# Reordering the front of a hybrid block: w_o's first two units, w_ada's last two column pairs, and which buffers short-lived tiles take

## The chip, the cores and the metric

The kernel runs on one core of a Trainium2 chip. The metric is the device time of one execution in microseconds (us). The engines are TensorE (PE: matrix products and transposes), VectorE (DVE), ScalarE (ACT), GpSimd (POOL) and SyncE (SP), which here issues nearly all the loads from HBM. Each engine works through its own list of instructions in order. An instruction that waits holds up everything behind it in that list.

## The reference, cut to what matters

The block has 256 tokens of width 1024. A conditioning vector goes through `w_ada` and gives six rows of 1024 numbers (shift, scale and gate for each half of the block). The first half is a mixer, the second a mixture of 32 experts of which each token uses four:

```python
c_act = jax.nn.silu(c)
ada = (c_act @ w_ada[l] + b_ada[l])[:, None, :]
sh_m, sc_m, g_m, sh_f, sc_f, g_f = jnp.split(ada, 6, axis=-1)
h = rms_norm(x, norm_mix_g[l]) * (1.0 + sc_m) + sh_m
...
merged = jax.nn.sigmoid(g_attn) * a_branch + jax.nn.sigmoid(g_conv) * c_branch
return merged @ w_o
...
x = x + g_m * mix
h = rms_norm(x, norm_ffn_g[l]) * (1.0 + sc_f) + sh_f
ffn = moe_ffn(h.reshape(B * S, D), router_w[l], router_b[l], ...)
x = x + g_f * ffn.reshape(B, S, D)
return rms_norm(x, norm_final_g)
```

`h` goes through one large projection `w_in` (attention latents, the inputs of a short convolution, and two gates `g_attn`, `g_conv` of 1024 columns each). `a_branch` is attention times `w_up_attn`, `c_branch` the convolution times `w_up_conv`. In `moe_ffn` the router's logits `h @ router_w + router_b` choose the experts, and every expert has `w_gu` (1024 x 2048) and `w_down` (1024 x 1024).

## The kernel before

**Two parts.** The front (the mixer up to the router and the gather for expert 0) lasts to about 242 us. After that the 32 experts follow one another. Each expert's weights are read once, as 2 MB tiles: four of `w_gu` and two of `w_down`, 12 MB for an expert.

**Buffers.** SBUF has 22 "narrow" buffers of 1 MB, numbered 0 to 21. After the front they are regarded as 11 "wide" buffers of 2 MB: wide buffer i is the narrow pair 2i and 2i+1. A wide tile can be loaded when the last reader of both its halves is done. `Slots.take` gives the buffer that was given back longest ago; `upto` (22, and 16 from unit 10 of the front on) makes it prefer the first so many. The wide tiles take the wide buffers in the order in which these were last given back, so the tiles that come last in this order are the ones whose narrow halves were in use longest.

**Loads.** SP issues all weights in one fixed order, `loads`: the front's units ("w": pieces of `w_in`, `w_up_conv`, `w_up_attn`, `w_o`, mostly 1 MB) and 16 chunks of `w_ada` of 1 MB ("a"), then the experts' tiles. `pump` issues the next load whenever more buffers are free than `spare`, and `spare` comes from a small table by unit. This fixes at which place in the program a load stands and which buffer it gets. On the chip the load then waits for that buffer's last reader, and all loads behind it wait too.

**Splitting.** Each front unit is used as two rounded parts. `split` takes two buffers, ScalarE writes the high part (L345), VectorE subtracts it from the raw weight for the low part (L346), and the raw buffer is given back. `unit()` returns the next unit and has the two after it split ahead of time. A product is then three matmuls (L334 to L336).

**w_ada in the front.** Of the sixteen chunks, (1, j) for j 0 to 7 are multiplied on TensorE (`ada_mm`, L250; 8 of them add up in one PSUM tile to row 1, which holds the mixer's gate `g_m` and the shift `sh_f`). The chunks (2, j) are multiplied and added on VectorE (L445, L448), and `ada_sum` (L455) adds over the partitions to row 2, with the scale `sc_f` and the gate `g_f`. `ada_next` handles the next chunk in the order of `ada_todo`: first all of row 1, then all of row 2.

**Order of the front after attention's scores.** Gates 4 to 7 (columns of `g_conv`) with attention in between; the convolution branch (`br`, two units); `gm_b` (`g_m` spread over the partitions, L462) and `sh_col` (the shift, transposed, L319), from which POOL computes `rwb` (router weights times shift) and VectorE its sum `rws` (L784); gates 0 to 3 (columns of `g_attn`) with an `ada_next` after each; `halves` of the attention output on ACT (L691) and POOL (L692); the attention branch's first unit, `ada_sum`, its second unit; `merge_t` (transposes of the merged branches, L799); `w_o` (`wo_mm`); the router.

**w_o.** It has four units of two row blocks each and four accumulators (two token tiles by two column halves). All four units are split before the first product. The first two units go into accumulator (0,0), then (0,1), (1,0) and (1,1); then come the router's constant terms (L934, L935, with `rws`), and the last two units, accumulator by accumulator, with the residual and the norm following each. A unit's buffers are given back (`drop`) after the last accumulator has used it.

## Time and profile before

| | us |
|---|---|
| median of 3 runs | 1167.49 (1165.46 to 1169.42) |
| the profiled execution's own time | 1166.59 |
| its span, first to last instruction | 1164.9 |
| TensorE busy in the span | 1067.3 (92%) |
| VectorE, ScalarE, GpSimd busy | 358.5, 152.8, 35.4 |
| moved by DMA | 457.66 MB, 393 GB/s over the span |

Busy shares are averages over two very different parts, the front and the experts, so the rows below go by stretch. The stretch 187 to 242 us is the front's end, 250 to 1135 us the experts.

### The profile page before, as it was taken

Reading aid. Unit: us, or ns where it says so; the run is one execution under the profiler, and the core shown is the slowest. Engines: PE = TensorE matmul, PEld = TensorE weight load, DVE = VectorE, ACT = ScalarE, POOL = GpSimd, SP = SyncE. Lnnn points to the kernel's source line nnn. Section 1 sums busy time; section 2 is a strip of 40 time slices with the busy share of each in tenths; the row PEclk is TensorE's granted clock in tenths of the full one; section 3 lists DMA queues with packets and bytes.
Section 4 is the critical chain, followed back from the end, with each engine's and each line's share of the span. In section 5 each row is a group of like instructions: output and inputs, shape, how many; then the busy total and the mean of one; then the engine's idle time right before and its main releaser. Section 6 shows DMA issues by size and latency. Waiting matters only on the chain. (4 is left out here: it accounts for less than half of the span.)

```text
span 1164.9 us, 11805 instructions
## 1 busy us (share of the span) xinstructions
PE 1067.3 (92%) x4914; PEld 488.5 (42%) x4914; DVE 358.5 (31%) x703; ACT 152.8 (13%) x261; POOL 35.4 (3%) x89
## 2 busy tenths in 40 slices
PE   5898998999999999999999879999888988898986
PEld 1887776744343343333433243343224322342323
DVE  3766688423221232122122121222112211211223
ACT  1544643311000010000000000010001000000001
POOL 1000002100000000000000000000000000000000
PEclk8898999979999999998999999999999999998999
DMA  9973686999999999999999999999999999999995
GB/s 354 393 271 136 231 325 240 352 429 429 424 430 426 428 428 415 428 428 427 428 427 429 429 423 429 427 427 429 426 428 428 428 428 428 427 428 426 428 419 180
DMA packets 48078, 457.66 MB, mean 393 GB/s; under 512 B 4939, under 2 KB 10088, under 8 KB 20628
## 3 DMA queue, kind: packets, MB, share of 16 engines
q1 hardware_dynamic: 47074, 456.06, 94.2%
q8 instruction: 41, 0.67, 0.2%
q0 software_dynamic: 272, 0.66, 0.2%
q10 hardware_dynamic: 674, 0.14, 0.1%
q14 instruction: 17, 0.14, 0.0%
HBM read 455.79 MB, written 1.05 MB: 392 GB/s over the span
## 5 line engine op out<-in xcount | busy, mean ns | idle before, releaser
L1074 PE MATMUL pg<-w,hsel 128*64 128x512 f32 x2048 | 459.4, 603 | 25.4 <-DMA w<-in_w_gu 25.2
L1074 PEld LDWEIGHTS pg<-w,hsel 128*64 128x64 f32 x2048 | 143.3, 139 | 325.9 <-issue 277.0
L1112 PE MATMUL pm<-w,aT 128*64 128x512 f32 (+1 forms) x1056 | 227.7, 582 | 9.1 <-DMA w<-in_w_down 7.6
L1092 DVE TENSOR_SCALAR ga<-pg 128x512 f32<-128x512 f32 x32 | 22.1, 692 | 459.2 <-PE pg L1074 442.4
L1112 PEld LDWEIGHTS pm<-w,aT 128*64 128x64 f32 x1056 | 74.0, 137 | 157.8 <-issue 133.9
L1093 ACT ACTIVATE sgm<-ga 128x512 f32<-128x512 f32 x32 | 20.2, 630 | 685.4 <-DVE ga L1092 685.4
L1118 DVE TENSOR_TENSOR yp<-gfx,pm 64x512 f32<-64x512 f32 x62 | 42.5, 685 | 196.5 <-PE pm L1112 195.9
L346 DVE TENSOR_TENSOR w<-w 128x2048 fp32r<-128x2048 f32 (+3 forms) x26 | 56.9, 2202 | 18.3 <-ACT w L345 18.0
L479 PE MATMUL mm<-w 128*128 128x512 f32 (+1 forms) x240 | 59.4, 408 | 2.7 <-ACT w L419 2.7
L1046 PE MATMUL pm<-oh,xs 128*128 128x256 f32 (+1 forms) x256 | 57.2, 383 | 4.7 <-DVE oh L1033 4.7
L1046 PEld LDWEIGHTS pm<-oh,xs 128*128 128x128 f32 x256 | 49.5, 200 | 15.9 <-issue 11.1
L334 PE MATMUL mm<-w 128*128 128x256 f32 (+1 forms) x160 | 54.2, 339 | 1.8 <-ACT w L691 1.2
L1137 PE MATMUL mm<-yp,s 128*128 128x512 f32 x120 | 54.9, 600 | 0.8 <-DVE yp L1118 0.8
L336 PE MATMUL mm<-w 128*128 128x256 f32 (+1 forms) x160 | 53.4, 334 | 1.7 <-DVE w L346 1.0
L479 PEld LDWEIGHTS mm<-w 128*128 128x128 f32 x240 | 48.3, 203 | 12.0 <-ACT w L419 3.8
L335 PE MATMUL mm<-w 128*128 128x256 f32 (+1 forms) x160 | 52.8, 330 | 0.0
L345 ACT ACTIVATE w<-w 128x2048 fp32r<-128x2048 f32 (+3 forms) x26 | 47.3, 1839 | 19.2 <-DMA w<-in_w_in 12.3
L1137 PEld LDWEIGHTS mm<-yp,s 128*128 128x128 f32 x120 | 22.1, 190 | 30.0 <-issue 27.5
L334 PEld LDWEIGHTS mm<-w 128*128 128x128 f32 x160 | 30.9, 193 | 8.4 <-issue 3.5
L250 PE MATMUL pa<-w,cact 128*32 128x512 f32 x128 | 21.1, 744 | 13.9 <-DVE rs_v L141 8.6
L1103 PE MATMUL pm<-ident,sgm 128*128 128x128 f32 x128 | 23.8, 308 | 10.4 <-ACT s L1066 7.9
L1223 POOL CAST sel<-id 128x256 fp32r<-128x256 f32 x32 | 12.7, 402 | 676.8 <-PE pg L1226 676.7
(283 smaller groups left out, 624.5 us busy)
## 6 DMA issues: line engine op xcount, KB each, us to landing
w<-in_w_gu SPq DMA_DIRECT2D x128, 2048.0 KB, 38.7
w<-in_w_down SPq DMA_DIRECT2D x62, 2048.0 KB, 39.1
w<-in_w_ada SPq DMA_DIRECT2D x24, 1024.0 KB, 6.5
w<-in_w_in SPq DMA_DIRECT2D x14, 1024.0 KB, 5.4
w<-in_w_o SPq DMA_DIRECT2D x4, 1024.0 KB, 9.0
w<-in_w_up_conv SPq DMA_DIRECT2D x2, 1024.0 KB
w<-in_w_up_attn SPq DMA_DIRECT2D x2, 1024.0 KB
w<-in_w_down SPq DMA_DIRECT2D x4, 512.0 KB, 32.3
```

Of the source, the lines that this page charges most:

```text
L334: TE.matmul(o, l[0], r[0], start=start, stop=False, skip_group_check=True)
L335: TE.matmul(o, l[0], r[1], start=False, stop=False, skip_group_check=True)
L336: TE.matmul(o, l[1], r[0], start=False, stop=stop, skip_group_check=True)
L345: S.activation(hi, raw, AF.Copy)
L346: V.tensor_tensor(lo, raw, hi, op=ALU.subtract)
L479: TE.matmul(ps[i][:, :n], hT[l][:, 4 * half + q, i * P:(i + 1) * P], u[r][:, q, :], start=(half == 0 and q == 0 and l == 0 and r == 0), st ...
L1046: TE.matmul(p[:, q, :], xs[:, i, fcols(2 * q2 + q)], oh[:, i, :n], start=(i == 0), stop=(i == NT - 1))
L1074: TE.matmul(pg[64 * g:64 * g + 64, n, :], hs[k // 4][:, k % 4, c0:c0 + CAP], w[:, f0:f0 + 512], start=False, stop=(k == NQ - 1), skip_grou ...
L1103: TE.transpose(p[:, q, :], a[:, q::4], ident)
L1112: TE.matmul(py[64 * h:64 * h + 64, :], aT[:, qa, 64 * g:64 * g + 64], w[:, h], start=(b == 0), stop=(b == 7), skip_group_check=True)
L1118: V.tensor_mul(yp[64 * k2:64 * k2 + 64, h * 512:(h + 1) * 512], gfx[hp, :], py[hp, :])
L1137: TE.matmul(acc[i][h], s2[:n, i * P:(i + 1) * P], yp[:n, h * 512:(h + 1) * 512], start=start, stop=False, skip_group_check=True)
```

## The change

1. `take` no longer goes by `upto` but prefers the first 16 buffers for everything that isn't a load. Once no loads are left in the list, it also prefers a buffer whose other half is held. `pump` counts only free buffers among the first `upto`, and the `spare` table is lower.
2. `ada_todo` goes (2,0), (1,0), (2,1), (1,1) and so on. SP's list of loads has the same kinds at the same places, so it is another chunk that is loaded at each "a".
3. `gm_b`, `sh_col` and `rwb` come after the attention branch; the sum `rws` after the fourth split of `w_o`.
4. `w_o`'s unit one goes into all four accumulators (with the second `merge_t` after the first two), then unit two into all four. The third unit is split after unit one's products, the fourth after unit two's. The last two units are used as before.

```diff
--- before.py
+++ after.py
@@ -79,8 +79,10 @@
             for i in range(len(since)):
                 pool.tile([P, size], F32, name="w", tag=f"w{i}", bufs=1)
 
-        def take(self, shape, dtype=F32):
-            i = min((i >= self.upto, c, i) for i, c in enumerate(self.since) if c is not None)[2]
+        def take(self, shape, dtype=F32, upto=16):
+
+            i = min((i >= upto, not loads and self.since[(i ^ 1) % len(self.since)] is not None, c, i)
+                    for i, c in enumerate(self.since) if c is not None)[3]
             self.since[i] = None
             t = self.pool.tile([P] + list(shape), dtype, name="w", tag=f"w{i}", bufs=1)
             self.held[id(t)] = (t, i)
@@ -93,7 +95,7 @@
             self.pump()
 
         def pump(self):
-            while loads and sum(c is not None for c in self.since) > self.spare:
+            while loads and sum(c is not None for c in self.since[:self.upto]) > self.spare:
                 loads.pop(0)()
 
     loads = []
@@ -365,19 +367,19 @@
         jobs += [mat_unit(w_up_attn, k) for k in range(2)]
         jobs += [mat_unit(w_o, k) for k in range(4)]
         raws, done, taken = [], [], [0]
-        ada_todo = [(g, j) for g in (1, 2) for j in range(8)]
+        ada_todo = [(g, j) for j in range(8) for g in (2, 1)]
         ada_raw, ada_ps = [], {}
 
         def ada_load(g, j):
             def issue():
-                w = slot([2048])
+                w = slot([2048], upto=narrow.upto)
                 load(w, ap_of(w_ada, g * 2048 + j * 6 * D, [[8 * 6 * D, P], [1, 2048]]))
                 ada_raw.append((g, j, w))
             return issue
 
         def raw_load(shape, src):
             def issue():
-                w = slot(shape)
+                w = slot(shape, upto=narrow.upto)
                 load(w, src)
                 raws.append((w, shape))
             return issue
@@ -398,7 +400,7 @@
         def unit():
             k = taken[0]
             taken[0] += 1
-            narrow.spare = {4: 7, 8: 6, 14: 5, 18: 4}.get(k, narrow.spare)
+            narrow.spare = {4: 6, 8: 4, 12: 3, 16: 2, 18: 1}.get(k, narrow.spare)
             if k == 10:
                 narrow.upto = 16
             ahead(k + 1 + LOOK[k])
@@ -771,17 +773,6 @@
         ada_next()
         next(br)
         ada_next()
-        gm_b = keep.tile([P, D], F32, name="gm_b", tag="bg2")
-        for h in range(2):
-            p = tpt()
-            spread_row(p, 1, h)
-            S.activation(gm_b[:, h * 512:(h + 1) * 512], p, AF.Copy)
-        V.tensor_copy(by_half(sh_col[:, 1, :]), halves_t(brow[1], tpt(), fcols)[:, 2:4, :, 0])
-        rwb = ft("rwb", [P, NE, NQ], 2, "pe0")
-        for q in range(NQ):
-            G.tensor_scalar(rwb[:, :, q], rw[:, q, :], sh_col[:, 1, q:q + 1], None, op0=ALU.mult)
-        rws = ft("rws", [P, NE])
-        V.reduce_sum(rws, rwb, axis=AX.X)
         for k in range(4):
             gate(k)
             if k == 3:
@@ -808,12 +799,21 @@
         ada_sum()
         wo = [unit(), unit()]
         next(br)
+        gm_b = keep.tile([P, D], F32, name="gm_b", tag="bg2")
+        for h in range(2):
+            p = tpt()
+            spread_row(p, 1, h)
+            S.activation(gm_b[:, h * 512:(h + 1) * 512], p, AF.Copy)
+        V.tensor_copy(by_half(sh_col[:, 1, :]), halves_t(brow[1], tpt(), fcols)[:, 2:4, :, 0])
         V.tensor_copy(by_half(a_col[:, 1, :]), halves_t(brow[2], tpt(), fcols)[:, 0:2, :, 0])
         V.scalar_tensor_tensor(a_col[:, 1, :], a_col[:, 1, :], 1.0, gffn, op0=ALU.add, op1=ALU.mult)
+        rwb = ft("rwb", [P, NE, NQ], 2, "pe0")
+        for q in range(NQ):
+            G.tensor_scalar(rwb[:, :, q], rw[:, q, :], sh_col[:, 1, q:q + 1], None, op0=ALU.mult)
+        rws = ft("rws", [P, NE])
         give(sg[1])
         mT = [slot([NQ, T], F32R), slot([NQ, T], F32R)]
         merge_t(0)
-        wo += [unit(), unit()]
         ss1 = keep.tile([P, NT, 2], F32, name="ss1")
 
         wps = [[None, None], [None, None]]
@@ -922,14 +922,20 @@
                 TE.matmul(ph[q // 4][:, q % 4, :], xs[:, i, fcols(q)], oh0[:, i, :],
                           start=(i == 0 and q % 4 == 0), stop=(i == NT - 1), skip_group_check=True)
 
-        wo_mm(0, 0, 0, 4)
-        wo_mm(0, 1, 0, 4)
+        wo_mm(0, 0, 0, 2)
+        wo_mm(0, 1, 0, 2)
         merge_t(1)
         give(sg[0])
         for q in range(NQ):
             G.tensor_scalar(rwa[:, q, :], rw[:, q, :], a_col[:, 1, q:q + 1], None, op0=ALU.mult)
-        wo_mm(1, 0, 0, 4)
-        wo_mm(1, 1, 0, 4)
+        wo_mm(1, 0, 0, 2)
+        wo_mm(1, 1, 0, 2)
+        wo.append(unit())
+        for i in range(NT):
+            for h in range(2):
+                wo_mm(i, h, 2, 4)
+        wo.append(unit())
+        V.reduce_sum(rws, rwb, axis=AX.X)
         p = tpt()
         TE.matmul(p[:, :NE], ones[0:1, :], rb, start=True, stop=False)
         TE.matmul(p[:, :NE], ones, rws, start=False, stop=True)
```

In the rows below, `w_...`, `mm_...`, `tp_...` and `pa_...` are tiles with their numbers; line numbers of the kernel after are 2 higher up to gate 0, and differ a little beyond. "x4" is four instructions.

**TensorE between the convolution branch and gate 0.** Before, the branch's last product is followed by `gm_b` (L462), `sh_col` (L319) and the gate's first products (L479):

```order
L335 MATMUL mm_1348<-w_1279,w_1217 128x512
L336 MATMUL mm_1348<-w_1278,w_1217 128x512
L462 MATMUL tp_1420<-brow12_145,ident_95 128x512
L462 MATMUL tp_1423<-brow12_145,ident_95 128x512
L319 MATMUL tp_1426<-ident_95,brow12_145 128x128 x4
L479 MATMUL mm_1443<-w_1337,w_339 128x512 x4
L479 MATMUL mm_1444<-w_1337,w_339 128x512 x4
```

Now it is followed by the chunk (1, 4) of `w_ada` (L252, raw buffer `w_1359`), and the gate:

```order
L337 MATMUL mm_1327<-w_1261,w_1204 128x512
L338 MATMUL mm_1327<-w_1260,w_1204 128x512
L252 MATMUL pa_697<-w_1359,cact_184 32x512 x4
L481 MATMUL mm_1401<-w_1316,w_339 128x512 x4
L481 MATMUL mm_1402<-w_1316,w_339 128x512 x4
L481 MATMUL mm_1401<-w_1316,w_340 128x512 x4
L481 MATMUL mm_1402<-w_1316,w_340 128x512 x4
```

`gm_b` and `sh_col` have moved behind the attention branch (L464, L321 there). A product that reads a freshly loaded chunk of `w_ada` stands in their place.

**TensorE in the first products of w_o.** Before, `w_1585` and `w_1625` (the high parts of units one and two) go into the same accumulator `mm_1705`; then the next accumulator follows:

```order
L334 MATMUL mm_1705<-w_1585,w_1668 128x512
L335 MATMUL mm_1705<-w_1586,w_1668 128x512
L336 MATMUL mm_1705<-w_1585,w_1669 128x512
L334 MATMUL mm_1705<-w_1625,w_1668 128x512
L335 MATMUL mm_1705<-w_1626,w_1668 128x512
L336 MATMUL mm_1705<-w_1625,w_1669 128x512
L334 MATMUL mm_1705<-w_1625,w_1668 128x512
L335 MATMUL mm_1705<-w_1626,w_1668 128x512
L336 MATMUL mm_1705<-w_1625,w_1669 128x512
L334 MATMUL mm_1718<-w_1585,w_1668 128x512
```

Now unit one (`w_1557`, `w_1558`) goes on to the next accumulator, `mm_1703`, and the second `merge_t` (L790) follows:

```order
L336 MATMUL mm_1696<-w_1557,w_1667 128x512
L337 MATMUL mm_1696<-w_1558,w_1667 128x512
L338 MATMUL mm_1696<-w_1557,w_1668 128x512
L336 MATMUL mm_1703<-w_1557,w_1667 128x512
L337 MATMUL mm_1703<-w_1558,w_1667 128x512
L338 MATMUL mm_1703<-w_1557,w_1668 128x512
L336 MATMUL mm_1703<-w_1557,w_1667 128x512
L337 MATMUL mm_1703<-w_1558,w_1667 128x512
L338 MATMUL mm_1703<-w_1557,w_1668 128x512
L790 MATMUL tp_1710<-ident_95,w_1403 128x128 x4
```

Unit two (`w_1601`, `w_1602`) comes after all 24 products of unit one.

**VectorE around the last splits.** Before, the low parts of units three and four (`w_1685`, `w_1689`) are made between the two `merge_t` (L803), and `rws` far ahead, before gate 0:

```order
L803 TENSOR_TENSOR w_1669<-tp_1670,w_1668 128x4x128
L803 TENSOR_TENSOR w_1669<-tp_1677,w_1668 128x4x128
L346 TENSOR_TENSOR w_1685<-w_1544,w_1684 128x2048
L346 TENSOR_TENSOR w_1689<-w_1547,w_1688 128x2048
L872 MEMSET lg_1695 128x2x8
L874 MEMSET m8_1697 128x16
L803 TENSOR_TENSOR w_1669<-tp_1731,w_1668 128x4x128
L803 TENSOR_TENSOR w_1669<-tp_1738,w_1668 128x4x128
```

Now both (`w_1747`, `w_1775`) stand behind the second `merge_t` (L794), with `rws` (L938) after them:

```order
L794 TENSOR_TENSOR w_1668<-tp_1710,w_1667 128x4x128
L794 TENSOR_TENSOR w_1668<-tp_1717,w_1667 128x4x128
L348 TENSOR_TENSOR w_1747<-w_1542,w_1746 128x2048
L348 TENSOR_TENSOR w_1775<-w_1551,w_1774 128x2048
L938 TENSOR_REDUCE rws_1666<-rwb_1657 128x32
L833 TENSOR_TENSOR jk_1795<-mm_1696,gm_b_1637 128x512
L834 TENSOR_TENSOR xs_90<-xs_90,jk_1795 128x512
```

`w_1747` is written into the buffer of `w_1558`, the low part of unit one, and `w_1775` into the buffer of `w_1601`, the high part of unit two. TensorE's product with `rws` (L941) comes right after unit two's last product, as before.

## Rows read from the trace of the kernel before

**Rows 1.** The page, the span in 40 equal slices: DMA busy tenths, GB/s.
```profile
DMA  9973686999999999999999999999999999999995
GB/s 354 393 271 136 231 325 240 352 429 429 424 430 426 428 428 415 428 428 427 428 427 429 429 423 429 427 427 429 426 428 428 428 428 428 427 428 426 428 419 180
```

**Rows 2.** The page, costliest groups of instructions: the experts' first matrix product.
```profile
L1074 PE MATMUL pg<-w,hsel 128*64 128x512 f32 x2048 | 459.4, 603 | 25.4 <-DMA w<-in_w_gu 25.2
```

**Rows 3.** Busy time by stretch: us, five engines, TensorE clock, DMA share, GB/s.
```profile
187.00:197.00 10.00, 8.27 (x33) 6.00 (x34) 8.43 (x9) 0.00 (x0) 0.00 (x0) 0.83 0.00 2
197.00:213.00 16.00, 15.44 (x76) 11.88 (x75) 8.80 (x13) 5.98 (x7) 9.02 (x12) 1.00 0.92 326
213.00:228.00 15.00, 14.77 (x77) 11.65 (x76) 6.95 (x22) 4.78 (x10) 0.00 (x0) 1.00 1.00 379
228.00:250.00 22.00, 17.98 (x87) 11.79 (x87) 9.17 (x32) 5.29 (x10) 3.97 (x6) 0.69 0.97 397
250.00:280.00 30.00, 30.00 (x150) 13.66 (x148) 7.34 (x24) 5.67 (x9) 0.40 (x1) 1.00 1.01 428
600.00:1135.00 535.00, 484.05 (x2092) 178.55 (x2089) 111.08 (x214) 24.67 (x46) 6.87 (x17) 0.99 1.01 427
```

**Rows 4.** Timeline of SP's queue, 1 MB loads: start, length, line, count.
```profile
112.61 0.34 SPq L374 DMA_DIRECT2D w<-in_w_ada  x1
```

**Rows 5.** Timeline of SP's queue: issues of the experts' 2 MB tiles.
```profile
174.76 0.43 SPq L1001 DMA_DIRECT2D w<-in_w_gu  x1
197.11 31.77 SPq L1001 DMA_DIRECT2D w<-in_w_gu  x7
228.98 1.07 SPq L1001 DMA_DIRECT2D w<-in_w_down  x2
234.15 22.35 SPq L1001 DMA_DIRECT2D w<-in_w_gu  x4
249.30 7.19 SPq L1001 DMA_DIRECT2D w<-in_w_gu  x3
```

**Rows 6.** Busy time by stretch, columns as in rows 3.
```profile
113.50:117.00 3.50, 3.50 (x18) 2.92 (x17) 2.45 (x10) 2.16 (x9) 0.00 (x0) 1.00 0.91 304
190.20:193.50 3.30, 3.30 (x10) 2.53 (x9) 3.27 (x4) 0.00 (x0) 0.00 (x0) 0.50 0.00 0
193.50:197.00 3.50, 3.50 (x17) 2.88 (x16) 3.15 (x5) 0.00 (x0) 0.00 (x0) 0.99 0.00 0
```

**Rows 7.** TensorE's timeline: start, length, line, tiles, count, [idle before <- releaser].
```profile
140.30 1.06 PE L250 MATMUL pa<-w,cact 128*32 128x512 f32 x8
154.00 1.88 PE L462 MATMUL tp<-brow,ident 128*128 128x512 f32 x4
156.10 22.02 PE L479 MATMUL mm<-w 128*128 128x512 f32 x96
...
179.32 0.50 PE L334 MATMUL mm<-w 128*128 128x512 f32 x1 [1.20 <-ACT w L691]
180.69 0.50 PE L336 MATMUL mm<-w 128*128 128x512 f32 x1 [0.63 <-POOL w L692]
...
188.73 1.07 PE L455 MATMUL pa<-w,ones 128*32 128x512 f32 x8 [2.76 <-DVE w L448]
...
198.72 0.50 PE L334 MATMUL mm<-w 128*128 128x512 f32 x1 [0.30 <-ACT w L802]
...
212.14 0.41 PE L935 MATMUL tp<-rws,ones 128*128 128x32 f32 x2
```

**Rows 8.** VectorE's timeline, 155 to 180 us.
```profile
160.11 0.42 DVE L784 TENSOR_REDUCE rws<-rwb 128x32 f32<-128x256 f32 x1 [2.89 <-POOL rwb L782]
174.19 2.29 DVE L346 TENSOR_TENSOR w<-w 128x2048 fp32r<-128x2048 f32 x1
176.39 2.35 DVE L448 SCALAR_TENSOR_TENSOR w<-w,cact 128x2048 f32<-128x2048 f32 x1
```

**Rows 9.** The page, DMA issues: count, KB each, median us to landing.
```profile
w<-in_b_gu POOLq DMA_DIRECT2D x4, 128.0 KB, 11.1
```

## The prediction

> **What bounds the kernel now.** First the page's slices [rows 1]: from the ninth slice on (233 us) the DMA engines are 9 of 10 busy or more and move 415 to 430 GB/s; only the last slice falls off. Then the costliest group [rows 2]: where TensorE waits in the experts' first product, it waits for a weight tile (25.2 of 25.4 us). The stretches say the same [rows 3]: DMA share 1.01 in 250 to 280 us and in 600 to 1135 us, at 428 and 427 GB/s. So after 250 us the time is the bytes left at 428 GB/s: 2.10 MB / 428 GB/s = 4.9 us for a tile. TensorE's delays there cost nothing. What can move the end is how far the loads have come when expert 0 gives back its first buffer, at 249.30 [rows 5], and when that is.
>
> In the front the queue is not full: from 187 to 197 us it moves nothing [rows 3], because SP's second tile waits for a buffer until 197.11 [rows 5]. That is the gap which the change could use. How far are the loads at 249.30? By the three stretches from 197 to 250 us [rows 3], 326 x 16 + 379 x 15 + 397 x 22 GB/s x us = 19.6 MB, less 0.5 MB of `b_gu` [rows 9], is 9.1 tiles; one more was issued at 174.76 [rows 5] and landed before the gap. That makes 10.1 at 250.0, 10.0 at 249.30, of 11 issued by then (1, 7, 2 and the first of the 4) [rows 5]. The buffers hold no more than 11. So the loads can gain one tile at most, whatever hole is filled, and everything else depends on when TensorE reaches expert 0.
>
> **The DMA's part.** In the changed program seven of the eleven wide buffers are pairs whose last readers are done before `w_o`'s second unit is through; the front's last load should land at about 186, and 7 x 4.9 us puts the seventh tile at about 221. The other four hold `w_o`'s last operands or the bias rows, as in the kernel before, where their loads were issued from about 228 to 234.15 [rows 5]. With y for the delay of TensorE's front they start at 228.1 + y; a load alone begins to move about 0.9 us after its issue (issued at 112.61 [rows 4], moving in 113.5 to 117.0 [rows 6]), so 229.0 + 4 x 4.9 = 248.6 + y: all eleven are there when the first buffer comes free at 249.3 + y. The queue then stands until 250.2 + y. At 250.2 the kernel before has 10.15 tiles. The gain is 0.85 x 4.9 = **4.2 us, less y**. Part of the old gap comes back, by the way: I expect none at 187 to 197, and one of 5 to 9 us ending near 229 + y.
>
> **y, the front on TensorE.** No matmul is added or taken away; the moved work is a wash by the end of `merge_t`. What counts are waits.
>
> Waits that go. The attention branch waited 1.20 us for ACT's and 0.63 us for POOL's halves [rows 7]; now two `w_ada` products (1.06 us each [rows 7]) stand ahead of it and cover them. `ada_sum` waited 2.76 us for VectorE's last chunk product [rows 7], behind five of its kind between 154 and 188 us at 2.35 us each [rows 8]; the new order spreads them back to 65 us, and VectorE should be done just before TensorE asks. After that wait the granted clock was 0.50 for 190.2 to 193.5 us and TensorE began 10 matmuls in 3.3 us there against 17 in the next 3.5 [rows 6]; at that rate it would have begun 16, so 6 matmuls of 0.21 us are lost, 1.2 us. Sum: 1.2 + 0.6 + 2.8 + 1.2 = 5.8 us.
>
> Waits that come.
> (a) The convolution's halves get the buffer that VectorE's subtraction in a split frees, and attention's last scores wait behind them on ACT: about half a subtraction of 2.29 us [rows 8], 1.0 us.
> (b) Chunk (1, 4) ahead of gate 0. Three chunk products fewer stand ahead and TensorE would be there about 3.2 us earlier than 154.0 [rows 7], at 150.8 with (a). The chunk's load waits for the split of gate 0's second unit. VectorE has the same splits and one more chunk product in this stretch, so I leave that split where it was, ending near 149.2. Issue to landing of a load alone is 4.4 us (112.61 [rows 4] to 117.0 [rows 6]): landing 153.5, wait 2.4 to 2.9 us. Gate 0 then starts at 154.4, against 156.10 [rows 7].
> (c) Chunk (1, 7) ahead of the attention branch. From (b) on twelve loads of 1 MB follow each other; 11 x 2.45 us (half a tile) after 153.5 is 180.4. TensorE is through gates 0 to 3 (22.02 us [rows 7]), one product among them and one behind at 154.4 + 22.0 + 2.1 = 178.5. Wait 1.9 us, at the least none if the loads run ahead.
> (d) `rws`. VectorE can make the fourth unit's low part only when unit two's last product has been read, since it goes into that buffer; then comes `rws`, and TensorE's product with `rws` is next in its list. That is 2.29 + 0.42 us [rows 8] and handovers, 2.9 us. Before, `rws` was ready 50 us ahead (160.1 [rows 8], used at 212.14 [rows 7]). Behind the waiting product stand `w_o`'s last two units, the residual, the router: nothing covers it.
> Sum: 1.0 + 2.4 + 1.9 + 2.9 = 8.2 us, so y = +2.4. A low clock after (d) like that after the 2.76 us of before would cost 1.2 more; the pair of 1.20 and 0.63 us shows none behind it, with matmuls at the full rate. One case on either side: I take half, y = 3.0, with 2.4 and 3.6 as its ends, and -1.9 if (b) and (c) are both covered.
>
> The Trainium skill (TensorE: Matmul & The Clock Gate, Part 1) has a gate that passes all or half of the clock by how busy TensorE has been recently, and not in step with the program, so that of two like waits one may be followed by the low clock and the other not. By that the sum is 1164.8 without it or 1166.0 with it. This trace has the two levels, 0.50 for 1.2 GHz and 1.00 for 2.4 GHz [rows 6]; which of them follows (d) no row shows.
>
> **The sum.** The profiled execution's own time is 1166.59 us, 0.9 below the median of the runs, 1167.49. 1166.6 - 4.2 + 3.0 = 1165.4; set against the median it is 1166.3. I say 1165.5, since the fast rivals hold more than the slow ones. About 0.3% (3.5 us) is what a measurement of this kernel can tell from no change, so this is "no difference", on the fast side.
>
> **Rivals.**
> 1. *The front gets earlier* (faster). For it: 5.8 us of waits go for certain, while (b) and (c) rest on the dates of loads, which this sum has to about 2 us, and the queue had room between 60 and 155 us (the third to sixth slice move 136 to 325 GB/s [rows 1]). If (b) and (c) are covered and the clock stays up, y = 8.2 - 4.3 - 5.8 = -1.9 and the time is 1166.6 - 4.2 - 1.9 = 1160.5, set against the median 1161.4. If one of the two is covered, 1162.6. It decides below y = 0.7. Against it: the split in (b) depends on VectorE, which got no faster there.
> 2. *A wide pair is held* (slower). Units three and four of `w_o` now sit in their raw buffers until after unit one and two. Were two more pairs kept by them than I count, nine tiles would be there at 249.3 + y, one less than before: 1166.6 + 4.9 + 3.0 = 1174.5. With one pair it is 1166.6 + 0.7 + 3.0 = 1170.3, no difference yet; it decides from the second. Against it: the tile order puts the pairs last used last, and no pair ahead of the eighth is one of theirs.
> 3. *The gap only moves* (no difference). If the loads gain nothing, because the bias rows' 128 KB pieces, 11.1 us to landing [rows 9], or the last four tiles stretch beyond 249.3 + y, the time is 1166.6 + y, 1169.6.
>
> **Chances.** My own sum 0.40 and rival 3 0.12 are no difference. Rival 1 has 0.37, of which 0.02 no difference (one wait covered, a low clock after the other). Rival 2 with two pairs has 0.08, and 0.03 are for (b) to (d) each bringing a low clock and more, y above 7.7. Faster 0.35, same 0.54, slower 0.11. The range goes from rival 1's end to rival 2's with one pair, 1160.5 to 1170.0; the sum's own is 1164.8 (no low clock) to 1166.9 (with it, against the median).
>
> **What would show it.** DMA share well above 0 in 187 to 197 us, and a gap that ends near 229 to 232. The first buffer after expert 0 given back at 251 to 253 instead of 249.3. TensorE waiting 2.5 to 3 us at the product with `rws` for VectorE, and no wait at `ada_sum`. A wait for a load of `w_ada` just ahead of gate 0. I am wrong if the first buffer comes back before 249.3 (then rival 1), or if fewer than eleven tiles are there at its first return (rival 2 or 3).

## The result, and the profile after

The changed kernel takes 1174.5 us (median of 9 runs, 1171.2 to 1176.4) against 1166.8 (9 runs of the kernel before on the same chip): ratio **1.0064 [1.0053, 1.0074]**, slower by about 7.5 us, where 1165.5 and "no difference" were forecast. The profiled run took 1175.23, which is 8.64 more than that of before.

Busy time by stretch of the kernel after (columns as in [rows 3]):

```profile
110.00:155.00 45.00, 41.68 (x222) 31.48 (x220) 33.10 (x54) 23.18 (x46) 1.27 (x1) 1.00 0.28 95
155.00:178.00 23.00, 22.36 (x92) 16.00 (x93) 11.70 (x6) 6.93 (x6) 0.00 (x0) 0.85 0.98 375
187.00:197.00 10.00, 10.00 (x44) 6.67 (x41) 6.36 (x5) 1.92 (x1) 0.00 (x0) 0.89 1.04 427
213.00:228.00 15.00, 12.56 (x44) 8.86 (x43) 5.58 (x5) 2.11 (x2) 2.30 (x4) 0.77 1.00 386
228.00:239.00 11.00, 10.77 (x60) 9.22 (x59) 5.46 (x21) 4.77 (x10) 0.00 (x0) 1.00 0.19 60
239.00:250.00 11.00, 9.03 (x53) 8.60 (x52) 7.53 (x23) 3.89 (x6) 3.57 (x5) 0.72 0.91 354
250.00:280.00 30.00, 28.71 (x135) 14.78 (x136) 9.02 (x33) 6.96 (x13) 0.80 (x2) 0.87 0.99 411
```

The gap of 187 to 197 us is gone (427 GB/s, 2 before [rows 3]). A new one stands in 228 to 239 (60 GB/s), as forecast, though some 7 us later than y = 3.0 puts it. What nobody forecast is the first row: in 110 to 155 us the loads move 95 GB/s. The same row of the kernel before has 209:

```profile
110.00:155.00 45.00, 44.87 (x242) 32.72 (x241) 28.78 (x53) 23.54 (x46) 1.36 (x1) 1.00 0.60 209
```

TensorE's timeline of the kernel after:

```profile
34.14 0.91 PE L481 MATMUL mm<-w 128*128 128x416 f32 x2 [1.18 <-ACT w L421]
...
131.38 1.58 PE L622 MATMUL tp<-w 96*128 96x128 f32 x8 [1.13 <-ACT w L670]
...
155.65 1.94 PE L252 MATMUL pa<-w,cact 128*32 128x512 f32 x8 [2.65 <-DMA w<-in_w_ada]
157.51 13.27 PE L481 MATMUL mm<-w 128*128 128x512 f32 x48
...
171.71 11.18 PE L481 MATMUL mm<-w 128*128 128x512 f32 x48
...
185.90 1.94 PE L252 MATMUL pa<-w,cact 128*32 128x512 f32 x8 [2.02 <-DMA w<-in_w_ada]
...
194.14 1.06 PE L457 MATMUL pa<-w,ones 128*32 128x512 f32 x8
...
204.66 0.50 PE L336 MATMUL mm<-w 128*128 128x512 f32 x1 [0.25 <-ACT w L793]
...
220.66 0.64 PE L941 MATMUL tp<-rws,ones 128*128 128x32 f32 x2 [2.44 <-DVE rws L938]
...
226.50 0.78 PE L464 MATMUL tp<-brow,ident 128*64 128x512 f32 x2
```

All four forecast waits are there at nearly their forecast sizes: (a) 1.13, (b) 2.65, (c) 2.02, (d) 2.44. The halves and `ada_sum` (194.14) wait for nothing. What is wrong are the dates. Gate 0 starts at 157.51 instead of 154.4, the chunk (1, 7) at 185.90 instead of 180.4, `w_o` at 204.66 instead of 198.2 (198.72 - 0.5). And three stretches run at the low clock: gates 0 and 1 take 13.27 us where the next two take 11.18, the clock is 0.50 again behind (c) (185.90 to 189.00), and the twelve products after `rws` take until 226.50.

A part of each of these dates is not the change's. TensorE's first product of `w_in` starts at 34.14, in the kernel before at 32.83. The same program starts there at different times in different executions: e1 below, which differs from the changed kernel only behind `w_o`'s second unit, has 32.27. So 1.3 us of every delay against the kernel before stood already at this product. The first product of `w_in` before, and in e1:

```profile
32.83 1.17 PE L479 MATMUL mm<-w 128*128 128x416 f32 x2 [1.18 <-ACT w L419]
32.27 0.91 PE L481 MATMUL mm<-w 128*128 128x416 f32 x2 [1.18 <-ACT w L421]
```

SP's queue of the kernel after:

```profile
132.99 18.02 SPq L376 DMA_DIRECT2D w<-in_w_ada  x2
...
163.00 0.38 SPq L383 DMA_DIRECT2D w<-in_w_up_attn  x1
...
187.06 52.43 SPq L1007 DMA_DIRECT2D w<-in_w_gu  x8
...
245.09 22.04 SPq L1007 DMA_DIRECT2D w<-in_w_gu  x4
259.94 7.19 SPq L1007 DMA_DIRECT2D w<-in_w_gu  x3
```

Of the two chunks at 132.99 the second, (1, 4), goes out only at 151.0 (132.99 + 18.02). SP's queue waits 15.3 us there for VectorE's subtraction in a split (L348), whose buffer the load takes (timeline of VectorE):

```profile
145.97 4.67 DVE L348 TENSOR_TENSOR w<-w 128x2048 fp32r<-128x2048 f32 x2 [3.13 <-ACT w L347]
...
217.98 2.29 DVE L348 TENSOR_TENSOR w<-w 128x2048 fp32r<-128x2048 f32 x1 [3.38 <-PE mm L338]
220.19 0.41 DVE L938 TENSOR_REDUCE rws<-rwb 128x32 f32<-128x256 f32 x1
```

The second of the two ends at 150.64, and SP issues the load 0.4 us later. For 18 us SP stands there, and every later load of the front stands behind it: the first of `w_up_attn` is issued at 163.00 (151.61 before). The last two rows are (d): the fourth split, then the sum, then TensorE. The bias rows' buffer is asked for at 245.09 (234.15 before), expert 0 returns its first buffer at 259.94 (249.30 before [rows 5]): y = **+10.6 us** instead of +3.0, or +9.3 without the later start.

### The profile page after: what moved, and what is told of

The parts are those of the page before. It is cut to its first block, busy times and chain, and to the rows that moved or that the text cites. A ratio compares the mean times of both kernels' runs of the same rounds, so it can differ in the third digit from the quotient of the medians.

```text
span 1173.6 us, 11809 instructions
## 1 busy us (share of the span) xinstructions
PE 1074.3 (92%) x4914; PEld 494.4 (42%) x4914; DVE 358.3 (31%) x703; ACT 152.7 (13%) x261; POOL 31.2 (3%) x89
## 3 DMA queue, kind: packets, MB, share of 16 engines
HBM read 455.79 MB, written 1.05 MB: 389 GB/s over the span
## 5 line engine op out<-in xcount | busy, mean ns | idle before, releaser
L1118 PEld LDWEIGHTS pm<-w,aT 128*64 128x64 f32 x1056 | 74.2, 137 | 154.4 <-issue 133.5
L348 DVE TENSOR_TENSOR w<-w 128x2048 fp32r<-128x2048 f32 (+3 forms) x26 | 56.9, 2200 | 34.3 <-ACT w L347 30.8
L481 PEld LDWEIGHTS mm<-w 128*128 128x128 f32 x240 | 49.8, 209 | 15.0 <-ACT w L421 3.9
L338 PE MATMUL mm<-w 128*128 128x256 f32 (+1 forms) x160 | 53.6, 335 | 0.1
L252 PE MATMUL pa<-w,cact 128*32 128x512 f32 x128 | 23.0, 806 | 18.8 <-DMA w<-in_w_ada 10.1
L336 PEld LDWEIGHTS mm<-w 128*128 128x128 f32 x160 | 31.1, 195 | 7.7 <-issue 4.4
L338 PEld LDWEIGHTS mm<-w 128*128 128x128 f32 x160 | 31.0, 194 | 3.8 <-DVE w L794 0.9
```

The lines of the kernel that those rows point to most:

```text
L336: TE.matmul(o, l[0], r[0], start=start, stop=False, skip_group_check=True)
L338: TE.matmul(o, l[1], r[0], start=False, stop=stop, skip_group_check=True)
L348: V.tensor_tensor(lo, raw, hi, op=ALU.subtract)
L481: TE.matmul(ps[i][:, :n], hT[l][:, 4 * half + q, i * P:(i + 1) * P], u[r][:, q, :], start=(half == 0 and q == 0 and l == 0 and r == 0), st ...
L1118: TE.matmul(py[64 * h:64 * h + 64, :], aT[:, qa, 64 * g:64 * g + 64], w[:, h], start=(b == 0), stop=(b == 7), skip_group_check=True)
```

## The experiments

Eighteen kernels ran, in five groups, each group beside the kernel before on its own chip. "First return" is the issue of the tile that takes expert 0's first buffer; "start" is the date of TensorE's first product of `w_in` (32.83 before). It varies by up to 3.7 us from execution to execution, so dates of two runs are compared less the difference of their starts. The last column is how much less the time rose than the first return, (first return - 249.30) - (profiled time - 1166.59); the start is in both and falls out.

| | ratio to before, 95% | start | first return | profiled time | kept |
|---|---|---|---|---|---|
| after | 1.0064 [1.0053, 1.0074] | 34.14 | 259.94 | 1175.23 | 2.0 |
| e1_rws_first | 1.0027 [1.0011, 1.0043] | 32.27 | 254.32 | 1169.18 | 2.4 |
| e2_ada_old | 0.9994 [0.9982, 1.0006] | 32.67 | 249.45 | 1165.12 | 1.6 |
| e3_slots_old | 1.0013 [0.9999, 1.0026] | 32.29 | 246.44 | 1168.59 | -4.9 |
| e4_wo_old | 1.0027 [1.0017, 1.0037] | 32.09 | 252.86 | 1168.23 | 1.9 |
| e5_fill | 1.0031 [1.0016, 1.0046] | 32.73 | 257.62 | 1172.41 | 2.5 |
| e6_ada_old_rws | 0.9972 [0.9959, 0.9985] | 32.01 | 245.85 | 1161.39 | 1.8 |
| e7_ada_pairs_rws | 1.0019 [1.0006, 1.0033] | 34.05 | 255.94 | 1170.58 | 2.7 |
| e8_ada_only | 1.0013 [1.0004, 1.0023] | 32.73 | 246.62 | 1168.81 | -4.9 |
| e9_fill_chunks | 1.0034 [1.0022, 1.0045] | 35.33 | 255.95 | 1171.05 | 2.2 |
| e10_ada_old_fill | 0.9982 [0.9973, 0.9992] | 31.75 | 247.85 | 1162.58 | 2.6 |
| e11_slots_only | 0.9990 [0.9979, 1.0000] | 31.66 | 247.92 | 1162.69 | 2.5 |
| e12_wo_only | 0.9992 [0.9983, 1.0002] | 35.29 | 252.73 | 1169.09 | 0.9 |
| e13_pump_all | 1.0029 [1.0017, 1.0041] | 32.77 | 254.12 | 1170.06 | 1.4 |
| e14_spare_old | 1.0058 [1.0044, 1.0072] | 32.29 | 255.54 | 1170.49 | 2.3 |
| e15_upto_old | 0.9965 [0.9951, 0.9979] | 31.85 | 244.91 | 1159.66 | 2.5 |
| e16_ada_old_pump | 0.9978 [0.9968, 0.9987] | 31.92 | 246.68 | 1161.97 | 2.0 |
| e17_after_upto_old | 0.9993 [0.9982, 1.0004] | 31.83 | 250.15 | 1164.95 | 2.5 |
| e18_ada_old_upto_old | 0.9986 [0.9975, 0.9997] | 34.79 | 251.44 | 1166.93 | 1.8 |

### The wait for rws, and the clock behind it: e1, e5

**e1_rws_first**: the sum ahead of the fourth split, so that VectorE has it done early.

```diff
+        V.reduce_sum(rws, rwb, axis=AX.X)
         wo.append(unit())
-        V.reduce_sum(rws, rwb, axis=AX.X)
```

> The sum rws is taken ahead of the fourth split instead of behind it; nothing else differs from the changed kernel (1174.5 us). Theory A (the loss is waits of TensorE, each followed by the low clock): the wait of 2.4 us at the product with rws goes, and the stretch of granted clock 0.5 that follows it (220.0 to 226.8 us, 3.4 us lost) goes with it. Expert 0 starts 5 to 6 us earlier and the time is about 1169. Rival B (the low clock is not tied to this wait): only the wait goes, about 1172. Rival C (the loads' dates, not TensorE, set the end): no change, 1174.

1.0027: 0.37% (4.3 us) of the loss goes. The rest is still there, and the second wait for a chunk is even larger (TensorE's timeline):

```profile
153.09 1.93 PE L252 MATMUL pa<-w,cact 128*32 128x512 f32 x8 [2.42 <-DMA w<-in_w_ada]
...
183.93 1.93 PE L252 MATMUL pa<-w,cact 128*32 128x512 f32 x8 [4.18 <-DMA w<-in_w_ada]
```

**e5_fill**: the changed kernel, with useless products in the place of the wait.

```diff
+        idle = tpt()
+        for n in (512, 512, 256):
+            TE.matmul(idle[:, :n], ident, gm_b[:, :n], start=True, stop=True)
```

> The wait for rws stays, but three extra products without use (two of 512 columns, one of 256, their result is read by nobody) stand ahead of it on TensorE and fill some 2.3 of the 2.4 us. Theory A: TensorE idles hardly at all, the granted clock stays 1.0 after it, and the 3.4 us of the low stretch come back: about 1171. Rival B: the clock falls at the same place all the same, 1174 to 1175. If even the added work costs, 1175.

The product with `rws` comes no earlier for it, counted from the start (219.56 less 32.73, against 220.66 less 34.14). TensorE's timeline, and the stretch around it:

```profile
219.56 0.41 PE L944 MATMUL tp<-rws,ones 128*128 128x32 f32 x2 [0.29 <-DVE rws L938]
```
```profile
210.00:228.00 18.00, 17.71 (x76) 12.87 (x75) 7.45 (x7) 3.61 (x6) 2.30 (x4) 1.00 0.93 357
```

No low clock there (1.00; 0.77 in 213 to 228 of the kernel after), and 1.0031, within the intervals as good as taking the wait away. So by the medians most of what (d) costs is the clock behind the wait; the intervals are too wide to say how much.

### Which part of the change makes the chunks late: e2, e3, e4, e7

**e2_ada_old**: the changed kernel with the old chunk order (the wait for `rws` stays).

```diff
-        ada_todo = [(g, j) for j in range(8) for g in (2, 1)]
+        ada_todo = [(g, j) for g in (1, 2) for j in range(8)]
```

> The chunks of w_ada go in the old order (all of row 1, then all of row 2); the rest of the change stays. Theory A: the waits for chunks (1,4) and (1,7) (2.7 and 2.0 us) and the low clock after them (3.2 and 1.9 us) go, 9.8 us; the wait at ada_sum (2.8 us) and its low clock (1.7 us) come back: about 5 us less, 1169 to 1170. Rival C' (lower spare table and first sixteen buffers make the loads late, whichever chunk it is): the first wait only changes its name, 1173 to 1175.

0.9994. No chunk is waited for, the halves are waited for again. The `rws` wait is the same to a hundredth, yet the clock stays up behind it (timeline and stretch):

```profile
212.18 0.41 PE L941 MATMUL tp<-rws,ones 128*128 128x32 f32 x2 [2.44 <-DVE rws L938]
```
```profile
208.00:222.00 14.00, 11.56 (x54) 8.44 (x52) 5.40 (x6) 2.48 (x7) 2.30 (x4) 1.00 1.02 359
```

**e3_slots_old**: part 1 undone as a whole (`take`, `pump`, `spare`, the loads' `upto`), the rest as changed.

> The buffers go as before (longest free, old spare table, pump counting all), the order of the chunks, of gm_b and of w_o as in the changed kernel. Theory A: chunk (1,4) still waits for a split's buffer or not, by the old table; if its load comes earlier than 151 us, both waits for chunks and their low clock go and the time is about 1166; the wait for rws may go too if the fourth unit's low part gets another buffer, then 1160 to 1163. Rival C': the same, as the buffers are the cause. If the chunks' order alone makes the waits, no change, 1174.

1.0013. No chunk and no `rws` is waited for, and the first return is 3 us earlier than before; but the time is 2 us longer: something else than the first return sets the end, as in e8 below.

**e4_wo_old**: `w_o` as before (all splits early, two units at a time), `rws` after the second `merge_t`.

```diff
+        wo += [unit(), unit()]
...
-        wo_mm(0, 0, 0, 2)
-        wo_mm(0, 1, 0, 2)
+        wo_mm(0, 0, 0, 4)
+        wo_mm(0, 1, 0, 4)
```

> The changed kernel with w_o split and used in the old order (all four units split first, rws summed after the second merge_t); buffers and order of chunks stay changed. Theory A: the waits for the chunks and the low clock behind them stay, the wait for rws and its low clock go, as in the run with rws first (3.7 us above the kernel before): 3 to 4 us above. Rival B2 (w_o's units, kept raw, hold the last wide pairs, so that the loads stand until TensorE is through): with them split early the loads stand for less, and it comes out 2 us or more below the run with rws first, 1 to 2 us above the kernel before.

1.0027, as e1, with 6.8 us of waits for chunks. `w_o`'s order in itself neither gains nor loses.

**e7_ada_pairs_rws**: e1 with rows 1 and 2 in order up to chunk 5, and only the last two pairs in turn.

```diff
-        ada_todo = [(g, j) for j in range(8) for g in (2, 1)]
+        ada_todo = ([(g, j) for g in (1, 2) for j in range(6)]
+                    + [(g, j) for j in (6, 7) for g in (2, 1)])
```

> Chunks 0 to 5 of row 1, then 0 to 5 of row 2, and only the last two pairs in turn; rws ahead of the fourth split. Theory A: the early loads and splits stand as with the old order, and two chunk products ahead of the attention branch cover its wait for the halves (3.4 us in the old-order run, with a low clock of 3.4 us lost behind it). If the last chunk's load is there in time, 5 to 7 us below the kernel before; if TensorE waits for it with a low clock behind, 1 to 2 us below. Rival (the order of the chunks does not matter, only the buffers): like the run with old order and rws first.

1.0019: a miss. TensorE waits 8.9 us for chunks, 7.5 of it in one wait. A chunk of row 1 that TensorE takes late is a chunk that TensorE waits for.

### Each part alone, and the best of it: e8, e11, e12, e6

**e8_ada_only**, **e11_slots_only**, **e12_wo_only**: the kernel before with the new chunk order and the moved `gm_b`, `sh_col`, `rwb` only; with part 1 only; with `w_o`'s order only (`rws` summed early, as before).

> The kernel before with only the new order of chunks, and gm_b, sh_col and rwb moved behind the attention branch (rws summed after the second merge_t); buffers and w_o as before. Theory A: the old buffers let the chunks' loads come in time (no wait of TensorE for w_ada was seen with the old buffers), ada_sum's wait and its low clock go: TensorE reaches expert 0 some 3 to 4 us earlier, but the loads, with the old buffers, are no further: between 1 us below and 2 us above the kernel before. Rival C (the chunks' order alone makes the waits): 4 us or more above.

> The kernel before with only the change to the buffers (first sixteen preferred, the pair rule, the lower spare table); order of chunks, gm_b and w_o as before. Theory A: no chunk stands ahead of gate 0, so no new wait for a load; the loads get ahead as in the run with the old order: 1 to 3 us below the kernel before, if VectorE's chain at ada_sum does not get longer. Rival C' (the new buffers alone make the splits and the loads late): 2 us or more above.

> The kernel before with only w_o's new order (unit one through all accumulators, then unit two, the third and fourth split later); rws is summed early as before, so nothing waits for it. Theory A: TensorE does the same work with no new wait; the raw units of w_o are held some 8 us longer, which with the old buffers can keep a wide pair: from no change to 3 us above the kernel before. Rival: the later splits of themselves make TensorE wait, 3 us or more above.

1.0013, 0.9990, 0.9992: none of them is worth 2 us either way; the loss is in the combination. In e8 TensorE is early (first return 246.62) and waits for no chunk, but SP stands before the wide tiles (stretch of e8):

```profile
213.00:228.00 15.00, 13.65 (x80) 11.75 (x79) 8.64 (x31) 7.40 (x15) 0.22 (x1) 1.00 0.46 171
```

171 GB/s against 379 before [rows 3]. The loads then lag so far that TensorE's early return is worth nothing: the last column, like e3's, is -4.9 where most others have about 2. So the new chunk order needs part 1's buffers, with which it loses at another place.

**e6_ada_old_rws**: e1 with the old chunk order.

> The old order of chunks together with rws ahead of the fourth split. The run with the old order alone was 0.1 us below the kernel before and still waited 2.4 us for rws, with no low clock behind it. Theory A: that wait goes, expert 0 starts 2.4 us earlier: 2 to 3 us below the kernel before, 1162.5 to 1163.5. Rival: the eleven buffers are full by then in any case, and the loads run into the next full stretch: 1 us below at the most.

0.9972, faster than both kernels.

### Is it the clock behind the waits? e9, e10

**e9_fill_chunks**: e1 with useless products ahead of the two chunks waited for, three and two.

> The changed kernel with rws first, and products without use (their result is read by nobody) ahead of the two products that waited for a chunk of w_ada: three of 512 columns (2.8 us) ahead of chunk (1,4), two (1.9 us) ahead of (1,7). The chunks land when they did. Theory A: TensorE is busy through most of both waits, the granted clock stays 1.0 after them, and the 5 us that the low clock took there in the run with rws first come back: from 3.7 us above the kernel before to 1 us below it, or 1 above where the loads are then full. Rival B: the clock falls at the same places, 3 to 4 us above, and 5 or more if the added work delays the products behind.

1.0034, no gain: a miss for the theory that the clock behind (b) sets the dates. The low clock after (b) is gone (the chunk's product takes 1.06 us, 1.93 in e1), and TensorE stands the longer at (c): 3.24 us behind two useless products of together 1.9, against 4.18 in e1.

```profile
156.06 1.06 PE L252 MATMUL pa<-w,cact 128*32 128x512 f32 x8
...
186.51 1.93 PE L252 MATMUL pa<-w,cact 128*32 128x512 f32 x8 [3.24 <-DMA w<-in_w_ada]
```

From chunk to chunk it is 30.5 us, as in the kernel after (185.90 - 155.65 = 30.3) and in e1 (30.8). The loads' dates set it.

**e10_ada_old_fill**: e6 with three useless products in the place of the wait for the halves.

> The kernel with the old order of chunks and rws first (3.2 us below the kernel before), with three products without use (2.8 us, read by nobody) ahead of the attention branch, where TensorE waited 1.2 us for ACT and 2.0 us for POOL and then lost 3.4 us to the low clock. Theory A: 3 us less, 6 us below the kernel before. Rival B: no change or slower by the filling, 2 to 3 us below. Rival (the loads are full by then): 4 us below at most.

0.9982, no better than e6. The low clock is gone there too, and some 8 us later TensorE waits for VectorE. First e10's TensorE and VectorE, then e6's:

```profile
183.87 1.07 PE L457 MATMUL pa<-w,ones 128*32 128x512 f32 x8 [2.55 <-DVE w L450]
...
178.05 5.76 DVE L450 SCALAR_TENSOR_TENSOR w<-w,cact 128x2048 f32<-128x2048 f32 x2
```
```profile
184.75 1.07 PE L457 MATMUL pa<-w,ones 128*32 128x512 f32 x8
...
178.84 5.75 DVE L450 SCALAR_TENSOR_TENSOR w<-w,cact 128x2048 f32<-128x2048 f32 x2
```

VectorE's chunk products end 0.8 us earlier in e10; more TensorE cannot have.

### Which of the buffer rules: e13 to e18

Each of e13 to e15 is e1 with one line of part 1 undone.

**e13_pump_all**:

```diff
-            while loads and sum(c is not None for c in self.since[:self.upto]) > self.spare:
+            while loads and sum(c is not None for c in self.since) > self.spare:
```

> The kernel with rws summed early (ratio 1.0027), and pump again counting all free buffers instead of the first sixteen; the lower spare table and take's preferences stay. Theory L (the count holds back the loads: the queue moves only 95 GB/s in 110 to 155 us, the chunks come late for that): the waits for chunks (1,4) and (1,7), together 6.6 us, shrink to under 2, the time falls by 4 to 6 us, to 0.995 to 0.999 of before. Theory S (the buffers, not the count, hold them back: a load waits on the chip for the last reader of its buffer, wherever it stands in the program): waits stay at 5 to 7 us and the ratio at 1.002 to 1.003.

1.0029. The queue moves 239 GB/s in 110 to 155 us and no chunk is waited for, as theory L had it, but the time stays, as theory S had it. TensorE waits for VectorE instead, 1.6 us at gate 0, 1.8 in a split product, and most at

```profile
187.61 1.52 PE L457 MATMUL pa<-w,ones 128*32 128x512 f32 x8 [3.08 <-DVE brow L444]
```

What the early chunks gain is lost further on. At `w_o`'s first product e13 is 4.3 us ahead of e1 (199.75 and 204.06), at the product with `rws` 4.4 (213.17 and 217.54), at the first return 0.2. From the product with `rws` to the next transposes (L842) e1 takes 7.40 us, e13 10.90: ScalarE's part of the fourth split is released only by a product of TensorE (L338), VectorE's part comes behind it, and TensorE waits 1.83 us for that and then runs at a low clock (0.66 in 218 to 223). TensorE and ScalarE of e13:

```profile
213.17 0.41 PE L941 MATMUL tp<-rws,ones 128*128 128x32 f32 x2
...
217.24 0.50 PE L337 MATMUL mm<-w 128*128 128x512 f32 x1 [1.83 <-DVE w L348]
...
212.94 1.92 ACT L347 ACTIVATE w<-w 128x2048 fp32r<-128x2048 f32 x1 [3.52 <-PE mm L338]
```

**e14_spare_old**: the old `spare` table.

> The kernel with rws summed early (ratio 1.0027), with the old, higher spare table and the count of the first sixteen kept. Theory L: a higher spare with the same count holds back the loads further; the waits for chunks grow to 8 us or more, ratio 1.004 or above. Theory S: the place in the program matters little; waits of 5 to 7 us, ratio 1.002 to 1.003.

1.0058, 8.1 us of waits for chunks. The lower table helps.

**e15_upto_old**: parts and other tiles that are no loads go by `upto` again, so they prefer the first sixteen buffers from unit 10 on, not from the start.

```diff
         def take(self, shape, dtype=F32, upto=16):
-
+            upto = self.upto
```

> The kernel with rws summed early (ratio 1.0027), where rounded parts and other tiles no longer prefer the first sixteen buffers before unit 10 (take goes by upto as in the kernel before); pump's count stays. Theory L: no change of the waits, ratio 1.002 to 1.004. Theory S: with the split parts spread over all 22 buffers again, loads find buffers whose readers are done earlier; waits for chunks under 3 us, ratio 0.998 to 1.000.

0.9965, the fastest of all. One wait of 1.1 us for a chunk is left.

**e16_ada_old_pump**: e6 with e13's line.

> The version with the old chunk order and rws summed early, which was 0.9972 of before, with pump counting all free buffers. It waits for no chunk. Theory L: earlier loads bring nothing to TensorE there, and the loads are full at the first return anyway; ratio 0.996 to 0.998. Theory S: the same. If it comes out at 0.995 or below, or at 0.999 or above, the count matters by way of the wide buffers' dates, which neither theory has.

0.9978, as e6: where no chunk is needed early, the count does nothing.

**e17_after_upto_old**: the changed kernel with e15's line and nothing else.

> The changed kernel with one thing undone: take goes by upto again, so that parts prefer the first sixteen only from unit 10 on. Theory P (take's preference delays the chunk loads, and the wait for rws with its low clock costs the rest, independently): from 0.9965 with rws summed early, plus 0.35% for the rws wait and its low clock, 0.999 to 1.001; chunk waits under 3 us, bias slot issued at 231 to 234 instead of 245.09. Rival Q (with rws late the buffers shift again and the chunks stay late): 1.003 to 1.006, chunk waits 4 us or more.

0.9993, as theory P has it. Its SP queue and TensorE, beside those of the kernel after above:

```profile
126.82 4.41 SPq L376 DMA_DIRECT2D w<-in_w_ada  x2
...
150.83 0.38 SPq L383 DMA_DIRECT2D w<-in_w_up_attn  x1
...
233.65 23.69 SPq L1007 DMA_DIRECT2D w<-in_w_gu  x4
```
```profile
151.83 11.18 PE L481 MATMUL mm<-w 128*128 128x512 f32 x48
...
177.30 1.06 PE L252 MATMUL pa<-w,cact 128*32 128x512 f32 x8 [1.18 <-DMA w<-in_w_ada]
...
210.42 0.41 PE L941 MATMUL tp<-rws,ones 128*128 128x32 f32 x2 [2.44 <-DVE rws L938]
```

The chunk (1, 4) goes out at 131.2 (126.82 + 4.41) instead of 151.0, without waiting for a split. Gate 0 starts 5.7 us earlier and the chunk ahead of the attention branch is multiplied 8.6 us earlier; 2.3 of both is the earlier start (31.83 against 34.14), so the line is worth 3.4 and 6.3 us there. With no wait at gate 0 there is no low clock behind it.

**e18_ada_old_upto_old**: e6 with e15's line.

> The version with the old chunk order and rws summed early (0.9972), with take going by upto again. It closes a square of chunk order against take's preference, all with rws summed early: 1.0027 (new order, first sixteen), 0.9972 (old order, first sixteen), 0.9965 (new order, by upto). Theory P (the preference hurts only by making chunk loads late that the new order needs early): no chunk is needed early here, so 0.996 to 0.998. Rival R (the preference costs time whatever the order): 0.993 to 0.995.

0.9986, a little above what theory P gave and far from rival R: with the old order the preference costs nothing.

## Why the prediction was wrong

The sum was -4.2 for the loads and +3.0 for the front. Measured: -2.0 and +10.6. Without the later start of the profiled execution the front is +9.3, and 9.3 - 2.0 = 7.3 is close to the 7.5 of the medians.

| | forecast | measured |
|---|---|---|
| to the first product of `w_in` (32.83 before) | 0 | +1.3 |
| from there to `w_o`'s first product (165.89 before) | -0.5 | +4.6 |
| from there to the product with `rws` (13.42 before) | +2.9 | +2.6 |
| from there to the first return (37.16 before) | +0.6 | +2.1 |
| first return, y | +3.0 | +10.6 |
| less what the loads keep | -4.2 | -2.0 |
| time | -1.2 | +8.6 |

**The step that failed is the date of the chunk loads in (b) and (c).** (b) named the right releaser, the split of gate 0's second unit, and the wait has its forecast size. Less the start's 1.3 us, TensorE is at this chunk and the chunk is there 0.9 us later than the 150.8 and 153.5 of the sum. The larger error is (c): it let twelve loads follow each other at 2.45 us, 26.9 us, and from chunk to chunk it took 30.3. A rate was taken from the experts' 2 MB tiles for the front's 1 MB pieces; in e17 these pieces move at 416 GB/s, which makes 1.05 MB / 416 GB/s x 11 = 27.8 us. And the kernel after moves only 375 in the same stretch, with two gaps, where SP issues its next pairs of loads late (169.64 and 175.62). The stretch in e17, then the two gaps in the kernel after:

```profile
155.00:178.00 23.00, 21.82 (x108) 15.71 (x106) 11.80 (x6) 10.27 (x10) 1.65 (x2) 1.00 1.02 416
```
```profile
170.00:172.00 2.00, 2.00 (x13) 0.77 (x12) 0.00 (x0) 1.69 (x3) 0.00 (x0) 1.00 0.66 154
176.00:178.00 2.00, 2.00 (x11) 1.65 (x10) 1.86 (x1) 0.11 (x1) 0.00 (x0) 1.00 0.86 205
```

The low clock behind (b) and (c) was not in the sum either. Behind (b) it costs nothing, since (c) waits for loads in any case (e9). Behind (c) the way to `w_o` takes 18.8 us (204.66 - 185.90) where the sum has 17.8 (198.2 - 180.4), with the clock at 0.50 in its first 3.1. A wait's size says little when both sides of it come late.

e17 shows which line sets these dates: with the old preference alone restored, the chunk is there before TensorE asks for it, and 0.71% of the time goes (1.0064 to 0.9993); in the pair without the wait for `rws` it is 0.62% (e1 to e15). The line does this together with `pump`'s count: e13 keeps it, counts all free buffers, and the chunk (1, 4) goes out at 129.5 (128.64 + 0.82). With both as changed, this load gets a buffer of that split. I had read from the order of instructions that the load waits for that split, and took this for a property of the new chunk order; it was one of the buffer rules. Two terms of the sum hang on it, (b) and (c), and the low clock behind (b).

**(d) had the right mechanism and a mis-sized term.** The wait is 2.44 us (2.9 forecast). The clock behind it was put at half of 1.2. From the product with `rws` to the next product after `w_o`'s third unit (226.50 - 220.66) it takes 5.84 us, where e17 takes 4.76 and the kernel before 3.19: 2.6 lost. At 2.4 and 2.6 (d) cost 1.5 us more than forecast in this run; by the medians, removing it is worth 0.37% (after to e1) or 0.28% (e17 to e15), 4.3 and 3.3 us, about the 3.5 of the sum. So of the 6.3 us by which y was off without the start, this is the small part. Undone in either order the two causes cost the same within the intervals: 0.71% and then 0.28%, or 0.37% and then 0.62%.

**What goes, went.** No wait at the halves, none at `ada_sum`, no low clock behind it.

**The loads' part was half right.** All eleven buffers are full at the first return to about a tenth of a tile, the gap moved to 228 to 239, and the loads cannot bank more lead than that. In the kernels with part 1, whole or but for one line of it, the last column is 1.4 to 2.7, however early or late TensorE is. It is not 4.2, since full buffers have a price that I put too low: after the first return the loads go at the pace of the returns. By its first return the kernel before has moved 297 GB/s x 249.30 us = 74.0 MB, the kernel after 292 x 259.94 = 75.9 MB, which is 1.9 MB or 4.4 us ahead. Then it lags twice, in the first ten us after the first return and again from 20 to 30 us after it. The kernel before, then the kernel after:

```profile
249.30:259.30 10.00, 10.00 (x48) 3.09 (x44) 0.00 (x0) 0.00 (x0) 0.00 (x0) 1.00 1.01 426
269.30:279.30 10.00, 10.00 (x50) 3.38 (x48) 0.34 (x2) 0.05 (x1) 0.00 (x0) 1.00 1.00 424
```
```profile
259.94:269.94 10.00, 10.00 (x48) 3.09 (x44) 0.00 (x0) 0.00 (x0) 0.00 (x0) 1.00 0.95 375
279.94:289.94 10.00, 10.00 (x50) 3.39 (x48) 0.33 (x2) 0.04 (x1) 0.00 (x0) 1.00 0.96 377
```

That is 0.5 MB each time, together 2.3 us, of which the sum had 0.9 (the queue standing once, until 250.2 + y). 4.4 - 2.3 = 2.1, about the 2.0 kept.

**The rivals.** Rival 1 (the front gets earlier) is what the change does without that one line and the late sum: in e15 the first return is 4.4 us earlier (1.0 of it the start) and the profiled time 1159.66. With the late sum and without the line the median is 1165.1 (e17), the forecast's 1165.5, though partly by two errors of opposite sign: y 0.9 (1.9 without its earlier start) and 2.5 kept, in place of 3.0 and 4.2. Rival 2 (a wide pair held) gave about the measured time for another reason: e4 without the late splits of units three and four is as e1. Wide tiles that wait for their pairs are what e3 and e8 show, which have the old `take`. Rival 3 (the gap only moves) is partly true. The 0.03 for "y above 7.7" was where the result lay, and it needed no chain of mishaps but one shared cause.

**What stays open.** Which buffer makes the fourth split of e13 late, so that early chunks and 239 GB/s gain nothing, was not tried by itself. How (d) divides into the wait and the clock is known from single traces only.

## What to carry to other kernels

A buffer rule is part of the schedule: when an in-order load queue takes its buffers from a shared pool, follow each load that a new order needs early to the instruction that frees its buffer, under the old rule and the new, before pricing the wait. Price dates, not waits: four waits of forecast size stood on dates that were up to 5 us late. Compare dates of two profiled executions only after taking off the difference of their starts (up to 3.7 us here). Where the end is bound by loads and the buffers are full, time follows the date of the first return nearly one for one (the last column is 1.4 to 2.7 in sixteen kernels), so a gain on TensorE counts only if neither the next load nor VectorE takes it back (e9, e10), and a combination of parts that are each worth nothing (e8, e11, e12) can still cost 0.6%.

## What the runs showed of the hardware

The same wait of 2.44 us at the same product was followed by three different clocks. In the kernel after the next twelve products ran low (0.50, 5.84 us for the stretch), in e17 part of them (4.76), in e2 none (1.00 in 208 to 222). The lost time was 2.6, 1.6 or none, so half of 1.2 us was no safe middle. The Trainium skill (TensorE: Matmul & The Clock Gate, Part 1) has a gate that goes by how busy TensorE was recently and is not in step with the program. The traces agree in so far as like waits had unlike clocks behind them.

With useless products in the place of a wait the clock stayed up in e5 (1.00 in 210 to 228), in e10 (1.00 in 178 to 182, 0.50 in e6) and in e9 at its first chunk. Only in e5, where no load and no VectorE stood behind, did the time follow.
